# All contraction tiles and the memory's values by Strassen's method in an fp32 decoder layer, its weight sums by DMA, and another order of its first loads

## The chip, the cores and the metric

The kernel runs on one core of one Trainium2 chip. The metric is the device time of one execution in microseconds (us): 1042.24 us, the median of three runs of the kernel before, which lay between 1041.75 and 1042.37. The engines that compute are TensorE (PE, with its weight load PEld), VectorE (DVE), ScalarE (ACT) and GpSimd (POOL); SyncE (SP) issues most transfers. Each engine runs its own queue of instructions in order, and semaphores tie the queues together.

## The reference

One decoder layer of 512 tokens of width 1024, all in float32: a half-step SwiGLU block (inner width 2816), a mixer, cross-attention into 256 memory tokens, and a second SwiGLU block, each followed by a residual and a layer norm.

```python
def _swiglu(h, w_in, w_out):
    gate, up = jnp.split(h @ w_in, 2, axis=-1)
    return (jax.nn.silu(gate) * up) @ w_out

def _memory_attention(h, mem, wq, wk, wv, wo):
    q = (h @ wq).reshape(b_, s_, XA_HEADS, XA_HEAD_DIM)
    k = (mem @ wk).reshape(b_, m_, XA_HEADS, XA_HEAD_DIM)
    v = (mem @ wv).reshape(b_, m_, XA_HEADS, XA_HEAD_DIM)
    s = jnp.einsum('bshd,bmhd->bhsm', q, k).astype(jnp.float32) * (XA_HEAD_DIM ** -0.5)
    p = jax.nn.softmax(s, axis=-1).astype(v.dtype)
    return jnp.einsum('bhsm,bmhd->bshd', p, v).reshape(b_, s_, D_MODEL) @ wo

# the layer
h = _layernorm(ALPHA * h + 0.5 * _swiglu(h, w_ffn1_in[l], w_ffn1_out[l]), ln1_g[l], ln1_b[l])
h = _layernorm(ALPHA * h + _parallel_mixer(...), ln2_g[l], ln2_b[l])
h = _layernorm(ALPHA * h + _memory_attention(h, mem, xa_wq[l], xa_wk[l], xa_wv[l], xa_wo[l]), ln3_g[l], ln3_b[l])
h = _layernorm(ALPHA * h + 0.5 * _swiglu(h, w_ffn2_in[l], w_ffn2_out[l]), ln4_g[l], ln4_b[l])
```

## The kernel before

**Three matmuls for one.** A float32 operand is split into a high part, rounded to the matmul's fast format, and the remainder as a low part. A product is then high times high, high times low, low times high: three matmuls that add up in one bank of the accumulator memory. Every weight block (128 rows of 1024 floats, 512 KB) is fetched by `wblock` (L76): SP issues the load into a tile `raw_...`, ACT casts it to `whi_...` (L67), DVE subtracts to get `wlo_...` (L68). There are seven buffers for the raw tiles, and seven for the high and low ones together. Activations are split in the same way.

**The stages, in the order of the program.** The first loads (L107 to L118) bring the eight pieces `x[k]` of the transposed input and the eight pieces `first[k]` of the first weights; all other work on PE waits for them. The FFN's first GEMM (`ffn`) makes gate and up by Strassen's method over the input's width, in matmuls of 256 columns. Its second GEMM (`strassen_gemm`, L317) has 22 contraction tiles of 128, held in six tiles `f1g0` to `f1g5` (`f2g...` in the second FFN). Twenty of them go through Strassen's method: five blocks for each half of the contraction (`KB1`, `KB2`), seven products of 5 blocks and 12 matmuls of 512 columns each, which accumulate in the banks u, v and w. The last two tiles are added by plain matmuls (`rest`, on the split tile `gs` and two weight blocks `ws`; 48 matmuls), and a bank x takes some of these. Seven products need sums of quarters on both sides: the left ones are made by DVE (`combine`, `left`), the right ones (t1, t2, t3, t4, sums of weight blocks) by transfers.

**The right sums** (class `Sums`, L268). POOL issues a transfer that copies a weight block to a scratch in DRAM, and a second one that adds another block to it on the way. A tiny POOL instruction (`seen`) that reads an instruction's result holds such a transfer back until that point of the program. For the first FFN all 20 copies and 20 adds are issued during its first GEMM (`step`); for the second one they are spread behind the 50 weight blocks of the mixer and the attention (`spread`, called through `behind`). They end there ahead of the last stage of the attention. In the output GEMM SP loads the sums like any weight block (`raw_f1t`, `raw_f2t`), without transfers of POOL beside it.

**The memory's values.** After the mixer and its layer norm come the keys of the memory (`pk`, `KM`) and then the values V = mem times wv (L899 to L914): two halves of 512 columns, four weight blocks each, 12 matmuls of 512 columns per block, 96 in all, into banks `vm`; ACT and DVE split each bank into `VM`. The split memory `mT` is there already. The query GEMM (weights `wxq`) follows.

**What sets the order.** The code is written once, and a scheduler at build time lays out each engine's queue. PE's queue is in order, so that an instruction that waits holds everything behind it. The same is true of DVE's, where splits, sums and residual adds share one queue, and of POOL's, where the power for a layer norm (`rstd`, L177) stands among the transfers.

Of the kernel before, what the change touches and what calls it, by code (L numbers as in the profile page):

```python
# [34 lines left out]
def layer_kernel(ctx: ExitStack, tc: tile.TileContext, a, out):  # L35
# [35 lines left out]

    last, behind = [None], []

    def wblock(src, name, stay=False):
        raw = raw4([P, 1024], f"raw_{name}")
        last[0] = nc.sync.dma_start(raw, src).ins  # L76
        if stay:
            both = b8([P, 2, 1024], F32R, f"ws_{name}")
            hi, lo = both[:, 0, :], both[:, 1, :]
        else:  # L80
            hi, lo = q4([P, 1024], f"whi_{name}"), q4([P, 1024], f"wlo_{name}")
        split(raw, hi, lo)
        for f in behind:
            f(hi)
        return hi, lo
# [22 lines left out]
    for k in range(KT):  # L108
        x = xf[k // 4][:, k % 4, :]
        nc.sync.dma_start(x, a["xT"][k])  # L110
        raw = raw4([P, 512], f"rawx{k}")
        (nc.scalar if k == 0 else nc.sync).dma_start(raw, a["first"][k])
# [152 lines left out]
    KB1, KB2 = [0, 1, 4, 5, 8], [2, 3, 6, 7, 9]  # L265
    NB = len(KB1)

    class Sums:  # L268


        def __init__(self, wsrc, name):
            self.w, self.name, self.T = wsrc, name, {}
            self.copies = [(p, b) for b in range(NB) for p in ("t1", "t3", "t2", "t4")]
            self.adds = list(self.copies)

        def copy(self, behind, of=("t1", "t3", "t2", "t4"), engine=None):

            todo = [c for c in self.copies if c[0] in of]
            if todo:
                p, b = todo[0]  # L280
                self.copies.remove(todo[0])
                T = self.T[p, b] = scr.tile([P, 1024], F32, name=f"{self.name}{p}{b}")
                with tc.issue_after(behind):
                    (engine or nc.sync).dma_start(T, self.w[p in ("t3", "t2"), (KB2 if p in ("t2", "t4") else KB1)[b]])

        def add(self, behind):

            if self.adds and self.adds[0] in self.T:
                p, b = self.adds.pop(0)
                x = {"t1": lambda: self.w[1, KB1[b]], "t3": lambda: self.w[1, KB2[b]],  # L290
# [4 lines left out]
        def spread(self, hi, over, count=[0]):  # L295

            total = 8 * NB
            n0, n1 = (total * (count[0] + i) // over for i in range(2))
            count[0] += 1
            for n in range(n0, min(n1, total)):  # L300
                seen = st.tile([P, 1], F32, tag="seen", name="seen")
                ins = nc.gpsimd.tensor_tensor(out=seen, in0=hi[:, 0:1].bitcast(F32), in1=mhalf[:, 0:1], op=ALU.mult).ins
                if self.copies and (n % 2 == 0 or n < 4):
                    self.copy(ins, engine=nc.gpsimd)
                else:
                    self.add(ins)

        def step(self, q, n):
# [3 lines left out]
            for _ in range(3 if n in (2, 4) else 2):  # L312
                self.add(ins)
            for _ in range(3 if n < 4 else 2):
                self.copy(ins, engine=nc.gpsimd)

    def strassen_gemm(wsrc, gt, S_, alpha, g, b, eps, name, final, pre):  # L317
        tiles = None
        stats = [st.tile([P, 2, 6], F32, tag=f"stats{t}", name=f"stats{t}", bufs=1) for t in range(NT)]
        lo, hi = slice(0, 256), slice(256, 512)  # L320
        quarter_ = {n: [gt[i][:, :, sl], gt[i + 2][:, :, sl], gt[4][:, i:i + 2, sl]]
                    for n, i, sl in (("a11", 0, lo), ("a12", 1, lo), ("a21", 0, hi), ("a22", 1, hi))}
        for n, i, sl in (("a12", 2, lo), ("a22", 2, hi)):
            quarter_[n][2] = gt[4][:, i:i + 2, sl]

        def left(p):

            T = []
            for i, x in enumerate(quarter_[p]):
                n = x.shape[1]  # L330
                t = (b8([P, 4, 2, 256], F32R, f"{name}{p}{i}") if n == 4
                     else wp.tile([P, 2, 2, 256], F32R, tag="raw", name=f"{name}{p}{i}", bufs=7))
# [4 lines left out]
        def combine(o, x, y, op):  # L337
            for i in range(3):
                nc.vector.tensor_tensor(out=quarter_[o][i], in0=quarter_[x][i], in1=quarter_[y][i], op=op)

        def right(p, stay=0):

            direct = {"b11": (0, KB1), "b21": (0, KB2), "b22": (1, KB2)}
            for i in range(NB):
                src = wsrc[direct[p][0], direct[p][1][i]] if p in direct else S_.T[p, i]
                yield wblock(src, f"{name}{p}{i}", i < stay)

        def block(t, i, w, T, ps, opens, ends):

            tsl = slice(t * P, (t + 1) * P)  # L350
            for j in range(2):
                k = 2 * i + j
                csl = slice(j * 512, (j + 1) * 512)
                ah, al = T[k][0][:, tsl], T[k][1][:, tsl]
                for n, (x, y) in enumerate(((ah, w[0]), (ah, w[1]), (al, w[0]))):
                    nc.tensor.matmul(ps, x, y[:, csl], start=opens and k == 0 and n == 0,  # L356
                                     stop=ends and j == 1 and n == 2, skip_group_check=True)

        def product(T, p, ps, opens):
            for i, w in enumerate(right(p)):  # L360
                for t in range(2):
                    block(t, i, w, T, ps[t], opens, False)
# [9 lines left out]
        assert not S_.copies and not S_.adds  # L372
        u, v, w = ([mm_ps(f"{name}{n}{t}") for t in range(2)] for n in "uvw")
        L = left("a11")
        s1 = b8([P, 2, 4, 256], F32, f"{name}s1")
        s1_ = sm.tile([P, 2, 256], F32, tag="s1", name=f"{name}s1_", bufs=2)
        quarter_["s1"] = [s1[:, 0], s1[:, 1], s1_]
# [15 lines left out]
        product(L, "b21", w, True)  # L393
        combine("a12", "a12", "a11", ALU.add)
        L = left("a12")

        T = b8([P, 2, 2, S], F32R, f"{name}gs")
        split(gt[5][:, :2, :], T[:, :, 0, :], T[:, :, 1, :])
        gs = [[(T[:, k, 0, sl], T[:, k, 1, sl]) for k in range(2)] for sl in (lo, hi)]
        product(L, "b22", v, False)  # L400
        ws = [wblock(wsrc[hf, 2 * NB], f"{name}{hf}_{2 * NB}", stay=True) for hf in range(2)]
# [9 lines left out]
        def rest(t, hf, ps, opens, scale):  # L411

# [653 lines left out]
```

## Time and profile before

| | value |
|---|---|
| median of three runs | 1042.24 us |
| the profiled execution | 1043.13 us, of which its span 1041.4 us |
| granted clock of TensorE, mean | 0.997 |
| ACT busy, of the span | 504.3 us (48%) |
| POOL busy, of the span | 95.0 us (9%) |
| bytes read and written in DRAM | 168.34 MB and 44.04 MB |
| POOL's transfers for the right sums | 30 from the second FFN's and 30 from the first FFN's weights, and 20 more between scratches |

The span is the profiled part of the execution, from its first instruction to its last; the 1.7 us around it are counted in the time, and taken as the same for both kernels. "L356" is line 356 of the kernel. In rows of a timeline the first number is the start, the second the time from the first start to the last end of the run of instructions in the row; in square brackets stands the time that the engine sat idle before, and what released it. A matmul's own duration in a row includes its drain; what one costs in a stream is the distance between two starts.

### The profile page before, as it was taken

The page shows a single profiled execution, that of the slowest core. Times are in us where ns is not written, and L with a number is a line of the kernel's source. Part 1 is how long each engine was busy: PE and PEld are TensorE (multiplying, and loading weights), DVE is VectorE, ACT ScalarE, POOL GpSimd, SP SyncE. Part 2 cuts the span into 40 slices and gives each one's busy share as a digit, 9 for nine tenths or more (in the row PEclk, how much of TensorE's full clock was granted, in tenths as well). Part 3 has the DMA queues.
Part 4 walks back from the last instruction along what each step waited for, and adds up shares of the span by engine and source line. Part 5 has one row for each costly group of instructions (what it writes and reads, how often), then busy time and mean ns, then how long its engine had stood idle before and what let it go on. Part 6 is the DMA issues. An engine that isn't in the chain of part 4 may idle for free. (4 is left out here: it accounts for less than half of the span.)

```text
span 1041.4 us, 17704 instructions
## 1 busy us (share of the span) xinstructions
PE 1025.7 (98%) x6910; PEld 929.4 (89%) x6910; DVE 825.4 (79%) x1334; ACT 504.3 (48%) x857; POOL 95.0 (9%) x167
## 2 busy tenths in 40 slices
PE   9999999999999999999999999999999999999996
PEld 7999999998887888879888988889999999988884
DVE  6999888789898545786786356589988888889795
ACT  5656555566554331334324345226555555566530
POOL 0112211200000111102303110010000000000000
PEclk9999999999999999999999999999999999999998
DMA  9377786585665446553929871403233332436751
GB/s 364 143 236 230 222 254 212 148 247 158 216 192 182 142 155 169 148 168 82 292 72 314 273 162 41 141 22 107 97 101 122 103 101 65 139 102 202 235 189 41
DMA packets 43300, 171.59 MB, mean 165 GB/s; under 512 B 6096, under 2 KB 7376, under 8 KB 40016
## 3 DMA queue, kind: packets, MB, share of 16 engines
q1 hardware_dynamic: 38592, 128.25, 36.9%
q0 software_dynamic: 4480, 41.95, 15.9%
q8 instruction: 54, 0.88, 0.3%
q10 hardware_dynamic: 144, 0.26, 0.1%
q14 instruction: 30, 0.25, 0.1%
HBM read 168.34 MB, written 44.04 MB: 204 GB/s over the span
## 5 line engine op out<-in xcount | busy, mean ns | idle before, releaser
L177 POOL TENSOR_TENSOR rstd<-ve,mhalf 128x1 f32<-128x1 f32 x16 | 14.8, 922 | 536.1 <-DVE ve L175 536.1
L538 PE MATMUL f1u<-xt,qf1s 128*128 128x256 f32 x480 | 60.7, 283 | 0.0
L538 PE MATMUL f2u<-xt,qf2s 128*128 128x256 f32 x480 | 60.7, 283 | 0.0
L538 PEld LDWEIGHTS f1u<-xt,qf1s 128*128 128x128 f32 x480 | 59.0, 192 | 0.0
L538 PEld LDWEIGHTS f2u<-xt,qf2s 128*128 128x128 f32 x480 | 59.0, 192 | 0.0
L68 DVE TENSOR_TENSOR wlo_wv<-raw_wv,whi_wv 128x1024 fp32r<-128x1024 f32 x12 | 14.7, 1224 | 23.8 <-PE pq L57 8.5
L538 PE MATMUL f1u<-xT,qf1a 128*128 128x256 f32 x240 | 32.1, 283 | 0.0
L538 PE MATMUL f2w<-xoT,qf2a 128*128 128x256 f32 x240 | 32.1, 283 | 0.0
L538 PE MATMUL f2u<-xoT,qf2a 128*128 128x256 f32 x240 | 32.1, 283 | 0.0
L538 PE MATMUL f1w<-xT,qf1a 128*128 128x256 f32 x240 | 32.1, 283 | 0.0
L538 PE MATMUL f1v<-xt,qf1s 128*128 128x256 f32 x240 | 30.7, 283 | 0.0
L538 PE MATMUL f1u<-xt,qf1a 128*128 128x256 f32 x240 | 30.6, 283 | 0.0
L538 PE MATMUL f1v<-xT,qf1s 128*128 128x256 f32 x240 | 30.4, 283 | 0.0
L538 PE MATMUL f2v<-xt,qf2s 128*128 128x256 f32 x240 | 30.4, 283 | 0.0
L538 PE MATMUL f2v<-xoT,qf2s 128*128 128x256 f32 x240 | 30.4, 283 | 0.0
L538 PE MATMUL f2u<-xt,qf2a 128*128 128x256 f32 x240 | 30.4, 283 | 0.0
L538 PEld LDWEIGHTS f1w<-xT,qf1a 128*128 128x128 f32 x240 | 30.3, 192 | 0.1
L538 PEld LDWEIGHTS f1u<-xT,qf1a 128*128 128x128 f32 x240 | 30.2, 192 | 0.0
L538 PEld LDWEIGHTS f2w<-xoT,qf2a 128*128 128x128 f32 x240 | 30.2, 192 | 0.0
L538 PEld LDWEIGHTS f2u<-xoT,qf2a 128*128 128x128 f32 x240 | 30.2, 192 | 0.0
L538 PEld LDWEIGHTS f1v<-xt,qf1s 128*128 128x128 f32 x240 | 29.6, 192 | 0.1
L538 PEld LDWEIGHTS f1u<-xt,qf1a 128*128 128x128 f32 x240 | 29.6, 192 | 0.0
(458 smaller groups left out, 3220.3 us busy)
## 6 DMA issues: line engine op xcount, KB each, us to landing
f1t<-in_w1out POOLq DMA_DIRECT2D x30, 512.0 KB, 8.2
f2t<-in_w2out POOLq DMA_DIRECT2D x30, 512.0 KB, 6.6
raw_f1t<-f1t SPq DMA_DIRECT2D x20, 512.0 KB, 4.1
raw_f2t<-f2t SPq DMA_DIRECT2D x20, 512.0 KB, 3.9
raw_f2g<-in_w2in SPq DMA_DIRECT2D x17, 512.0 KB, 3.7
raw_f2u<-in_w2in SPq DMA_DIRECT2D x17, 512.0 KB, 3.7
raw_f1u<-in_w1in SPq DMA_DIRECT2D x15, 512.0 KB, 7.2
raw_f1b<-in_w1out SPq DMA_DIRECT2D x15, 512.0 KB, 4.8
```

What stands on the lines that cost most here:

```text
L68: nc.vector.tensor_tensor(out=lo, in0=src, in1=hi.bitcast(F32), op=ALU.subtract)
L177: nc.gpsimd.tensor_tensor(out=rstd, in0=ve, in1=mhalf[:, 0:1], op=ALU.pow)
L538: nc.tensor.matmul(o, q[:, w, wsl], x[k][r], start=opens and k == 0 and n == 0, stop=ends and k == 3 and n == 2, skip_group_check=True)
```

## The change

1. **First loads.** SP issues `first[k]` ahead of `x[k]`; before it was `x[k]` first, and `first[0]` was issued from ACT's queue. In DVE's queue the low part of `first[0]` now stands ahead of the cast of `x[0]`, and PE's four products of the high parts stand at the front.
2. **The FFN's output GEMM.** All 22 tiles go through Strassen's method. There is a sixth block for each half of the contraction that has one tile: the two halves of weight block 10. `rest`, `gs`, `ws` and bank x are gone. A product is 66 matmuls, a GEMM 462 (before 468).
3. **Right sums.** Each sum has six blocks, the last one half as large. t1, t2 and t3 are made during the FFN's first GEMM as before, 2 adds and 2 copies a step; the six copies and six adds of t4 now stand inside the output GEMM, one behind every second weight block (`one_behind`, `pace`). In the mixer and the attention the sums for V come first (8 copies, 8 adds), then those of the second FFN as far as the stages reach, behind four of five weight blocks and behind none in the stage of V; what is left by then is issued in the second FFN. POOL issues 116 of them in place of 80.
4. **The memory's values.** V goes through Strassen's method: tokens, contraction and columns are halved, seven products of 2 weight blocks and 6 matmuls a block, 84 in place of 96. The 8 weight blocks become 14, eight of which are sums read back from the scratch. The memory is loaded a second time in float32 (`memf`, 1 MB), DVE makes four sums on it and ACT and DVE four splits of those, and the results pass through the copies c11, c12 and c22.

```diff
-        nc.sync.dma_start(x, a["xT"][k])
         raw = raw4([P, 512], f"rawx{k}")
-        (nc.scalar if k == 0 else nc.sync).dma_start(raw, a["first"][k])
+        nc.sync.dma_start(raw, a["first"][k])
+        nc.sync.dma_start(x, a["xT"][k])
...
-    KB1, KB2 = [0, 1, 4, 5, 8], [2, 3, 6, 7, 9]
+    FFN_BLOCKS = [0, 1, 4, 5, 8, (10, 0)], [2, 3, 6, 7, 9, (10, 1)]
...
+        def actions(self):
+            c, a, seq = len(self.copies), len(self.adds), []
+            while a:
+                if c and a - c < 4:
+                    seq.append(self.copy)
+                    c -= 1
+                else:
+                    seq.append(self.add)
+                    a -= 1
+            return seq
...
+    todo_behind, pace = [], [0, 1, 2]
+    def one_behind(hi):
+        pace[0] += 1
+        if todo_behind and pace[0] * pace[1] % pace[2] < pace[1]:
+            seen = st.tile([P, 1], F32, tag="seen", name="seen")
+            todo_behind.pop(0)(nc.gpsimd.tensor_tensor(out=seen, in0=hi[:, 0:1].bitcast(F32), in1=mhalf[:, 0:1],
+                                                       op=ALU.mult).ins)
...
-        assert not S_.copies and not S_.adds
+        todo_behind.extend(S_.actions())
+        pace[:] = 0, 1, 2
...
-        ws = [wblock(wsrc[hf, 2 * NB], f"{name}{hf}_{2 * NB}", stay=True) for hf in range(2)]
-        def rest(t, hf, ps, opens, scale):
-            block(t % 2, 0, ws[hf], gs[t // 2], ps, opens, True)
-            add(t, hf, ps, scale)
         for t in range(2):
-            rest(t, 0, w[t], False, False)
-            rest(t, 1, v[t], False, False)
+            for hf, ps in enumerate((w[t], v[t])):
+                add(t, hf, ps, False)
+                stats_of(t, hf)
...
         for t in range(2):
             add(2 + t, 1, u[t], False, ALU.subtract)
-            rest(2 + t, 1, mm_ps(f"{name}x{t}"), True, False)
+            stats_of(2 + t, 1)
         for t in range(2):
             for i, x in enumerate(T4):
-                block(t, i, x, L, u[t], False, False)
-            rest(2 + t, 0, u[t], False, True)
+                block(t, i, x, L, u[t], False, i == nb - 1)
+            add(2 + t, 0, u[t], True)
+            stats_of(2 + t, 0)
...
-    behind.append(lambda hi: sums2.spread(hi, 50))
+    sums_v = Sums(a["wv"], "vm", [0, 1], [2, 3])
+    todo_behind += sums_v.actions() + sums2.actions()
+    pace[:] = 0, 4, 5
...
+    mem_sum("s1", "a21", "a22", ALU.subtract)
+    mem_sum("a21", "a11", "a21", ALU.subtract)
+    mem_sum("a11", "s1", "a11", ALU.subtract)
+    mem_sum("a12", "a12", "a11", ALU.add)
+    vu, vv, vw = (mm_ps(f"vm{n}") for n in "uvw")
+    mem_product(vu, mem_left("a11", (0, 0)), "b11", True, False)
+    c11 = part_of_v("c11", vu)
+    mem_product(vv, mem_left("s1"), "t1", True, False)
+    c22 = part_of_v("c22", vv)
+    mem_product(vu, mem_left("a11"), "t2", False, False)
+    c12 = part_of_v("c12", vu)
+    mem_product(vw, mem_left("a12", (1, 0)), "b21", True, True)
+    nc.vector.tensor_tensor(out=c11, in0=c11, in1=vw, op=ALU.add)
+    values_done(0, 0, c11)
+    mem_product(vv, mem_left("a12"), "b22", False, True)
+    nc.vector.tensor_tensor(out=c12, in0=vv, in1=c12, op=ALU.subtract)
+    values_done(0, 1, c12)
+    mem_product(vu, mem_left("a21"), "t3", False, False)
+    nc.vector.tensor_tensor(out=c22, in0=c22, in1=vu, op=ALU.subtract)
+    values_done(1, 1, c22)
+    mem_product(vu, mem_left("a22", (1, 1)), "t4", False, True)
+    values_done(1, 0, vu)
+    pace[:] = 0, 4, 5
```

Three places in the queues. A row is the line, the operation, what it writes and reads, and the shape; the number behind a name's underscore only counts the program's tiles.

**DVE at the start of the first FFN's output GEMM, before.** `f1a110` and `f1a111` are the low parts of the first product's left operand (of `f1g0` and `f1g2`), `wlo_f1b112` is the low part of its third weight block, and `f1g5` is the last tile of the inner activations.

```order
L525 TENSOR_TENSOR f1g5_275<-f1sg_2616,f1u_2621 128x256
L68 TENSOR_TENSOR wlo_f1b112_2992<-raw_f1b112_2989,whi_f1b112_2991 128x1024
L525 TENSOR_TENSOR f1g5_275<-f1sg_2687,f1u_2692 128x256
L68 TENSOR_TENSOR f1a110_2942<-f1g0_270,f1a110_2942 128x4x256
L68 TENSOR_TENSOR f1a111_2945<-f1g2_272,f1a111_2945 128x4x256
```

The same place after the change; `f1a113` is the left operand of the new half block.

```order
L534 TENSOR_TENSOR f1g5_275<-f1sg_2606,f1u_2611 128x256
L68 TENSOR_TENSOR f1a110_2936<-f1g0_270,f1a110_2936 128x4x256
L534 TENSOR_TENSOR f1g5_275<-f1sg_2677,f1u_2682 128x256
L68 TENSOR_TENSOR f1a111_2939<-f1g2_272,f1a111_2939 128x4x256
L68 TENSOR_TENSOR f1a113_2945<-f1g5_275,f1a113_2945 128x256
L68 TENSOR_TENSOR wlo_f1b112_2994<-raw_f1b112_2991,whi_f1b112_2993 128x1024
```

The first left operand now stands ahead of the third weight block's low part, which was in front of it.

**DVE in the stage of V, before.** `wlo_wv10` is the low part of the first weight block of the second column half, `vm00` a bank of the first.

```order
L68 TENSOR_TENSOR wlo_wv03_5994<-raw_wv03_5991,whi_wv03_5993 128x1024
L68 TENSOR_TENSOR wlo_wv10_6018<-raw_wv10_6015,whi_wv10_6017 128x1024
L68 TENSOR_TENSOR wlo_wv11_6040<-raw_wv11_6037,whi_wv11_6039 128x1024
L68 TENSOR_TENSOR VM0_5923<-vm00_5925,VM0_5923 128x512
L68 TENSOR_TENSOR wlo_wv12_6061<-raw_wv12_6058,whi_wv12_6060 128x1024
L68 TENSOR_TENSOR VM1_5924<-vm01_5926,VM1_5924 128x512
```

After the change, the front of the stage: the last key `KM1` (from the last product ahead of V), the last of the four sums on `memf`, the splits of s1 and a11, and then the first weight blocks of the sums t1 and t2 (`wvt10` to `wvt20`).

```order
L68 TENSOR_TENSOR KM1_5119<-pk_5975,KM1_5119 128x256
L942 TENSOR_TENSOR memf_6004<-memf_6004 128x4x128
L68 TENSOR_TENSOR vls1_6040<-vs1_6006,vls1_6040 128x4x128
L68 TENSOR_TENSOR vla11_6069<-memf_6004,vla11_6069 128x4x128
L68 TENSOR_TENSOR wlo_wvt10_6046<-raw_wvt10_6043,whi_wvt10_6045 128x1024
L68 TENSOR_TENSOR wlo_wvt11_6058<-raw_wvt11_6055,whi_wvt11_6057 128x1024
L68 TENSOR_TENSOR wlo_wvt20_6075<-raw_wvt20_6072,whi_wvt20_6074 128x1024
```

And its end, with the last weight blocks (t3 and t4) and the results; `c22` reads the bank u (`vmu`) into which the last product, t4, adds next.

```order
L966 TENSOR_TENSOR c11_6038<-c11_6038,vmw_6013 128x512
L68 TENSOR_TENSOR wlo_wvb221_6143<-raw_wvb221_6140,whi_wvb221_6142 128x1024
L68 TENSOR_TENSOR wlo_wvt30_6161<-raw_wvt30_6158,whi_wvt30_6160 128x1024
L68 TENSOR_TENSOR VM0_6002<-c11_6038,VM0_6002 128x512
L969 TENSOR_TENSOR c12_6096<-vmv_6012,c12_6096 128x512
L68 TENSOR_TENSOR wlo_wvt31_6173<-raw_wvt31_6170,whi_wvt31_6172 128x1024
L68 TENSOR_TENSOR wlo_wvt40_6188<-raw_wvt40_6185,whi_wvt40_6187 128x1024
L68 TENSOR_TENSOR VM0_6002<-c12_6096,VM0_6002 128x512
L972 TENSOR_TENSOR c22_6067<-c22_6067,vmu_6011 128x512
L68 TENSOR_TENSOR wlo_wvt41_6200<-raw_wvt41_6197,whi_wvt41_6199 128x1024
```

Between the last key and `c22` stand 11 splits of a weight block and, with `c22`, 10 operations on 512 columns; where these rows lie, the weight blocks were before split with a result between them now and then.

**POOL ahead of the attention's layer norm, before.** A `seen` reads the high part of a weight block, and the transfer behind it is held to that; the layer norm's first `rstd` is the last row.

```order
L302 TENSOR_TENSOR seen_6771<-whi_xo0_0_6767,mhalf_264 128x1
L293 DMA f2t24_6120<-f2t14_6023 64x2048
L302 TENSOR_TENSOR seen_6808<-whi_xo0_1_6804,mhalf_264 128x1
L293 DMA f2t44_6242<-f2t24_6120 64x2048
L177 TENSOR_TENSOR rstd_6971<-ve_6969,mhalf_264 128x1
```

The same place after the change; `whi_f2g0` and `whi_f2u0` are the first weight blocks of the second FFN, whose loads SP issues there.

```order
L322 TENSOR_TENSOR seen_7028<-ws_xo1_1_7025,mhalf_264 128x1
L281 DMA f2t23_7030<-in_w2out 16x8192
L322 TENSOR_TENSOR seen_7037<-ws_xo1_2_7034,mhalf_264 128x1
L290 DMA f2t22_6609<-f2t12_6226 64x2048
L322 TENSOR_TENSOR seen_7056<-whi_f2g0_7052,mhalf_264 128x1
L281 DMA f2t14_7058<-in_w2out 16x8192
L322 TENSOR_TENSOR seen_7066<-whi_f2u0_7062,mhalf_264 128x1
L290 DMA f2t13_6880<-in_w2out 64x2048
L174 TENSOR_TENSOR rstd_7100<-ve_7098,mhalf_264 128x1
```

The transfers behind the first and second weight block of the output projection are gone from there, and others now stand behind its last blocks and behind the second FFN's first two.

180 lines of the change are left out of this document (96 added, 84 removed).

## The prediction

> **What bounds the kernel now.** I read the page's busy times first, then the chain that ended last, then windows of the stages that the change touches, and last the timelines at the places where PE stops.
>
> ```profile
> PE 1025.7 (98%) x6910; PEld 929.4 (89%) x6910; DVE 825.4 (79%) x1334; ACT 504.3 (48%) x857; POOL 95.0 (9%) x167
> PE 10%; DVE 0%; DVEq 0%; issue 0%
> PE f2u L356 5%; PE f2v L356 3%; PE f2w L356 2%; PE f2x L356 0%; DVE h L183 0%; DVE h L180 0%; DVE stats L415 0%; DVE h L367 0%; DVEq L1062 0%; DVE mv L173 0%; DVE ve L175 0%
> ```
>
> PE is busy in 98% of the span, and the part of the chain that the page follows runs through PE's matmuls of the last output GEMM. So a matmul that goes is time won, as long as what feeds PE keeps up. The price of a matmul comes from the old stage of V, where PE never stopped:
>
> ```profile
> L909 PE MATMUL vm<-whi_wv,mT x32: 389/389/396, 557.5 to 578.6; 128*128 128x512 f32 x32
> L911 PE MATMUL vm<-whi_wv,mT x32: 389/389/389, 558.0 to 579.1; 128*128 128x512 f32 x32
> 557.00:580.00 23.00, 23.00 (x108) 19.24 (x107) 12.58 (x13) 10.88 (x14) 5.89 (x13) 1.00 1.04 348
> ```
>
> The first and the last of its 96 matmuls start 21.6 us apart, so one costs 21.6 / 95 = **0.227 us**. The window's columns are PE, PE's loads, DVE, ACT, POOL, the granted clock, the DMA share and GB/s: DVE works 12.6 of 23 us, while the DMA engines are full.
>
> **The FFN's output GEMMs: matmuls, and the stall at the start.** 468 matmuls become 462, in two FFNs: 12 x 0.227 = **-2.72 us** if nothing takes PE's place.
>
> ```profile
> 230.63 0.40 PE L356 MATMUL f1u<-wlo_f1b,f1a 128*128 128x512 f32 x1
> 231.77 0.73 PE L356 MATMUL f1u<-whi_f1b,f1a 128*128 128x512 f32 x2 [0.74 <-DVE f1a L68]
> 924.39 0.40 PE L356 MATMUL f2u<-wlo_f2b,f2a 128*128 128x512 f32 x1
> 925.53 0.73 PE L356 MATMUL f2u<-whi_f2b,f2a 128*128 128x512 f32 x2 [0.75 <-DVE f2a L68]
> 229.03 1.22 DVE L68 TENSOR_TENSOR wlo_f1b<-raw_f1b,whi_f1b 128x1024 fp32r<-128x1024 f32 x1
> 230.16 0.41 DVE L525 TENSOR_TENSOR f1g<-f1sg,f1u 128x256 f32<-128x256 f32 x1
> 230.49 2.36 DVE L68 TENSOR_TENSOR f1a<-f1g,f1a 128x1024 fp32r<-128x1024 f32 x2
> ```
>
> At the start of each GEMM PE steps from 230.63 to 231.77 and from 924.39 to 925.53: 1.14 in place of 0.227, a loss of 0.91. It waits for the low part of the first left operand, and DVE had the third weight block's low part in front of that (229.03 to 230.16 by the starts, 1.13). The change puts the weight block behind. That is more than the loss, so both stalls go: **-1.83 us** (at worst 0, if DVE reaches this place later by as much). Late next is the second left operand, which follows by two operations and is needed four matmuls on at the earliest.
>
> DVE's own load in this stage grows. Prices by the distance of starts: 1.13 for 1024 columns, 0.33 for 256 (230.16 to 230.49), 0.61 for 512 (567.88 to 568.49, below). Added per FFN: 1.5 blocks' splits (1.7), seven pieces of left operands (2.3), four pieces of sums (1.3); gone: `gs` (1.1) and two residual adds (1.2): +3.0.
>
> ```profile
> 231.50:323.00 91.50, 91.23 (x406) 75.61 (x407) 83.30 (x92) 49.95 (x53) 1.99 (x2) 1.00 0.61 194
> 924.40:1014.70 90.30, 89.55 (x395) 73.85 (x394) 82.54 (x89) 48.89 (x51) 1.85 (x2) 1.00 0.62 198
> 1011.97 2.72 PE f2x L356 x12
> ```
>
> DVE goes from 82.5 of 90.3 us to some 85.5 of 89.4: 96%. It still fits, with the buffers of three and a half blocks between it and PE, but not everywhere. The weakest place is in front of the t4 product. Before, PE had the 12 matmuls into bank x there (2.72 us in the chain) while DVE emptied bank u; now t4 goes into u at once. The add of 512 columns (0.69) has only the last three matmuls of the other bank (0.68) beside it, and what remains is the matmul's drain (0.39 - 0.23 = 0.16) and what DVE is behind by. I take 0.25 per FFN, **+0.5 us** (0 to 2: at the upper end the whole add and a share of the last splits stand open).
>
> **The memory's values.** Ideally 84 x 0.227 = 19.1 in place of 21.8. But DVE has the longer list.
>
> ```profile
> 567.88 0.69 DVE L68 TENSOR_TENSOR VM<-vm,VM 128x512 fp32r<-128x512 f32 x1 [0.57 <-ACT VM L67]
> 568.49 1.22 DVE L68 TENSOR_TENSOR wlo_wv<-raw_wv,whi_wv 128x1024 fp32r<-128x1024 f32 x1
> 545.00:557.00 12.00, 12.00 (x102) 11.93 (x101) 10.80 (x19) 6.58 (x12) 5.73 (x8) 1.00 0.80 253
> 557.71 0.37 ACT L67 CAST KM<-pk 128x256 fp32r<-128x256 f32 x1 [1.56 <-PE pk L58]
> ```
>
> Let the first matmul of V start at T. DVE is at work 10.8 of the 12 us ahead of it, so the new sums on `memf` can't be finished early. The last key's cast on ACT ends about T + 0.6 (557.71 + 0.37 against 557.5). From there DVE's queue holds the key (0.33), ten operations of 512 columns (6.1) and 11 splits (11 x 1.13 = 12.4) up to and with `c22`: T + 19.4. The low part of `wvt10` is the fifth operation; it is done at T + 0.6 + 0.33 + 3 x 0.61 + 1.22 = T + 4.0, while PE has used its first 12 matmuls and one more at T + 2.95: a stall of 1.05. `c11`, `c12` and `c22` each wait for a product that PE ends later by this, so I put it on DVE's list: `c22` at T + 20.5. Only then can t4's 12 matmuls enter bank u: 20.5 + 2.72 + drain of about 0.2 = T + 23.4, against 21.8: **+1.6 us**, though 12 matmuls are gone. If DVE's waits are hidden, it is T + 22.3, +0.5; if PE waits for nothing at all, -2.7, which DVE's list excludes. The other way, loads that come late decide:
>
> ```profile
> raw_wxq<-in_wq SPq DMA_DIRECT2D x8, 512.0 KB, 13.0
> raw_wv<-in_wv SPq DMA_DIRECT2D x6, 512.0 KB, 5.6
> 530.00:545.00 15.00, 15.00 (x86) 12.54 (x85) 13.21 (x28) 4.11 (x10) 1.54 (x2) 1.00 0.04 11
> q1 hardware_dynamic: 38592, 128.25, 36.9%
> q0 software_dynamic: 4480, 41.95, 15.9%
> ```
>
> SP's queue moved 128.25 MB in 36.9% of 1041.4 us on all 16 DMA engines: 1.57 us for a block of 512 KB. Old V fetched 8 blocks while POOL's sums filled the engines, and `raw_wv` landed 5.6 us after its issue. Now no sum is issued here, but 14 blocks take 22.0 us of all engines: nearly the whole stage. The 1 MB of `memf` and the first blocks can come ahead of it, where the share was 0.04 in 530 to 545. I take no loss, and one late block, 4 us (the 5.6 less what a buffer ahead covers), as the upper end.
>
> **The attention's layer norm (LN3).** Two sums of POOL now lie beside the loads of the second FFN's first blocks.
>
> ```profile
> 677.82 0.69 DVE L517 TENSOR_TENSOR f2s<-raw_f2u 128x512 f32<-128x512 f32 x1 [3.19 <-DMA raw_f2u<-in_w2in]
> 678.43 0.68 DVE L243 SCALAR_TENSOR_TENSOR h<-h,xops 128x512 f32<-128x512 f32 x1
> 682.88 0.63 PE L195 MATMUL trh<-ident,h 128*128 128x128 f32 x4 [0.69 <-DVE h L183]
> raw_f2u<-in_w2in SPq DMA_DIRECT2D x5, 512.0 KB, 4.5
> ```
>
> DVE waits 3.19 us for `raw_f2u`, the residual add `h` stands behind it in the queue, and PE waits 0.69 for the norm of that `h`; whatever delays it further adds to this wait one for one. POOL's 80 transfers took 15.9% of 1041.4 = 166 us, 2.07 each. One such beside the load moves the chain DVE, `h`, `trh` by 0 to 2.1; two by 4.1 at most. I take half of one, **+1.0 us**, because the landing of 4.5 us holds queueing that may absorb some. In the Trainium skill, "DMA: Bandwidth & Descriptors", section "Queues, rings and completion order", each DMA engine takes turns between the queues that have work, a packet at a time. By that rule a load meets one sum packet for each of its own: the load's 1.57 us would double, this term would be +1.6, and the sum 0.6 above mine. The landings of 13.0 us beside sums and 4.5 us without agree with sharing, though more of SP's loads were queued in the first.
>
> **The first loads.**
>
> ```profile
> 4.91 0.43 DVE L67 CAST xT<-xf 128x512 fp32r<-128x512 f32 x1 [3.90 <-DMA xf<-in_xT]
> 5.11 0.62 ACT L67 CAST qx<-rawx 128x512 fp32r<-128x512 f32 x1 [2.44 <-DMA rawx<-in_first]
> 5.98 0.68 DVE L68 TENSOR_TENSOR qx<-rawx,qx 128x512 fp32r<-128x512 f32 x1
> 6.72 0.50 PE L58 MATMUL first<-xT,qx 128*128 128x512 f32 x1
> ```
>
> Before, PE's stream is closed from its third matmul on, at 6.72, as if it had started without gaps at 6.72 - 2 x 0.23 = 6.27. Now `first[0]` lands first, near 4.9; ACT casts it to 5.5, DVE's low part takes to about 6.15, and only then comes the cast of `x[0]` (0.43): start at 6.6, with four high products to cover the rest. **+0.35 us** (-0.4, if the first transfer lands earlier now that none is issued beside it, to +0.9).
>
> Transfers in the first FFN's first GEMM become fewer by those of t4; nothing waited there, so nothing is won.
>
> **Sum:** -2.72 - 1.83 + 0.5 + 1.6 + 1.0 + 0.35 = -1.1. From the profiled execution's 1043.13 (span 1041.4, 1.7 around it, taken as unchanged) that gives 1042.0. That execution lies 0.89 above the median of 1042.24, so the forecast for a median is **1041.1 us**. About 0.2% (2.1 us) is what a measurement of this kernel can tell from no change, so this is "the same".
>
> **Rivals.**
> *Cheaper V and hidden tails.* PE is fed as the buffers allow: V costs +0.5, LN3 and the t4 start nothing: -2.72 - 1.83 + 0.5 + 0.35 = -3.7, 1038.5. For it speaks that DVE and ACT are free for 10 of 23 us in the old V; against it, the order of DVE's list.
> *The output GEMM falls behind: slower.* Its 12 sums now share the DMA engines with 42 loads. In a product of 15 us SP fetches 5.5 blocks' worth and POOL makes 1.7 transfers: 5.5 x 1.57 + 1.7 x 2.07 = 12.2 us of all engines, 81%, where the window shows 0.61. PE has about five raw blocks ahead (the left operands hold the others of the seven buffers), 5 x 2.72 us less some 2.2 for the block's split: **11.4 us of landing time is the point from which it decides**. `raw_wxq` took 13.0 beside sums, but at a share of 1.04; that speaks against it. With DVE at 96% nothing is caught up: 1.7 us for each of two blocks, about 3.5 per FFN: 1041.1 + 7 = 1048.
> *The change does little of what it says*, because DVE at 96% in the output GEMMs hands PE each block just in time and the time of the 12 matmuls goes into waits: the sum without its first term, 1041.1 + 2.7 = 1043.8. It ends within the measurement.
>
> **How the numbers follow.** Forecast 0.45 (1041.1), cheaper 0.25 (1038.5), little gained 0.11 (1043.8), slower 0.19 (1048). Faster by over 0.2% means under 1040.2: nearly all of the cheaper case and the lower end of the forecast, 0.23 + 0.08 = 0.31. Slower means over 1044.3: nearly all of the slower case, and a late load in V, 0.18 + 0.03 = 0.21. The rest is 0.48. The range goes from the cheaper case, half a microsecond lower for the bound of the first loads (1038.0), to the forecast with the late load of V or with one FFN falling behind (1041.1 + 4, rounded up: 1045.2). The forecast's own range is 1039.7 to 1042.9.
>
> **What would show it.** Right: no step over 0.4 us at the start of the two output GEMMs, matmuls of 512 columns fewer by 24; in V two stalls of about 1 us, by `wlo_wvt10` and by `c22`, and DVE nearly closed between them; one longer wait for `raw_f2u` ahead of `trh`. Wrong: loads in the output GEMMs that land after 10 us or more with PE waiting for `whi_f1b` or `whi_f2t` (the slower case); V with 20 us or less (the cheaper one); stalls spread over the output GEMMs that end at DVE (the one with little gained).

## The result, and the profile after

| | before | after |
|---|---|---|
| median of five runs | 1042.32 us | 1048.65 us (1045.56 to 1049.13) |
| ratio | 1 | 1.0055 (95% interval 1.0043 to 1.0066) |
| the profiled execution, its span | 1043.13, 1041.4 us | 1045.56, 1043.8 us |

The changed kernel is slower by 6.3 us, outside the range of the prediction. Its profiled execution is the shortest of the five; the others took 1048.2 to 1049.1. What the trace of 1045.56 shows is told first, and the 3 us to the others with the first experiment.

The page of the changed kernel, with each engine's busy time, and its line on POOL's transfer queue (packets, MB, share of 16 DMA engines):

```profile
PE 1023.6 (98%) x6886; PEld 924.7 (89%) x6886; DVE 842.4 (81%) x1377; ACT 517.9 (50%) x892; POOL 156.8 (15%) x232
q0 software_dynamic: 6784, 54.53, 21.2%
```

PE's busy time fell by 2.1 us and its matmuls from 6910 to 6886, the 24 that the prediction named, while the time rose: something else came. To find it, the span is cut at the first matmul of each stage. The table has, in us, the kernel before, two traces of the changed one (the second is from e1), and some of the experiments that follow: e3 and e4 are built on the kernel before, e5 to e9 on the changed one.

| stage | before | e3 | e4 | after, 1st | after, 2nd | e5 | e6 | e7 | e9 |
|---|---|---|---|---|---|---|---|---|---|
| until the first matmul on loaded data | 5.78 | 4.97 | 5.24 | 5.25 | 5.24 | 5.31 | 5.25 | 5.30 | 5.29 |
| first products | 22.43 | 22.44 | 22.41 | 22.64 | 22.77 | 21.86 | 22.26 | 22.20 | 22.63 |
| FFN 1, first GEMM | 201.72 | 201.89 | 201.72 | 201.85 | 201.87 | 201.88 | 201.84 | 201.84 | 201.84 |
| FFN 1, output GEMM | 111.43 | 110.63 | 110.71 | **107.82** | **108.50** | 108.38 | 108.59 | 108.16 | 108.38 |
| mixer and keys | 216.15 | 216.16 | 216.16 | 216.80 | 216.75 | 216.76 | 216.78 | 216.74 | 216.77 |
| V, queries, attention | 90.47 | 90.47 | 90.51 | **92.56** | **92.66** | 92.73 | 92.61 | 90.46 | 89.43 |
| output projection, norm (LN3) | 49.75 | 49.78 | 49.84 | **51.89** | **54.45** | 49.61 | 49.65 | 49.58 | 49.59 |
| FFN 2, first GEMM | 225.95 | 225.95 | 225.95 | 225.96 | 225.95 | 226.38 | 225.95 | 225.96 | 226.42 |
| FFN 2, output GEMM | 106.93 | 106.93 | 106.93 | **105.65** | **105.40** | 105.39 | 105.61 | 105.65 | 105.65 |
| from the last matmul's start to the end | 10.73 | 8.13 | 13.66 | **13.36** | **13.35** | 13.35 | 8.04 | 7.95 | 8.04 |
| span | 1041.36 | 1037.36 | 1043.13 | 1043.79 | 1046.94 | 1041.65 | 1036.58 | 1033.83 | 1034.06 |

In the second trace the output GEMMs are shorter by 2.93 and 1.53 us, and the mixer's stage is longer by 0.60; some 0.4 of that are four small matmuls (`trh`) of a late norm, which now stand behind the mixer's first matmul. V lost 2.2, the norm behind the attention 2.1 and 4.7, and the end of the program 2.6.

e3 and e4 show how far one trace of the kernel before can be trusted, since they leave its code as it is up to the second FFN. They agree with it to 0.2 us in each stage up to there but two. They start earlier, and their first output GEMM takes 110.63 and 110.71 us in place of 111.43. The same place in the timelines of the kernel before and of e4:

```profile
324.36 0.63 PE L195 MATMUL trh<-ident,h 128*128 128x128 f32 x4 [0.91 <-issue]
323.08 0.63 PE L195 MATMUL trh<-ident,h 128*128 128x128 f32 x4 [0.20 <-issue]
```

The wait of 0.91 us in the middle of the GEMM is 0.20 in e4, and 0.14 in e3. So 0.7 to 0.8 of the 2.93 us, and PE's earlier start, differ between executions of the same code and can't be put down to the change. Against e3 and e4 the output GEMMs with the mixer won 3.1 us in the second trace.

**The output GEMMs.** A timeline of PE of the changed kernel, at the places of the two stalls of 0.91 us:

```profile
229.97 0.40 PE L367 MATMUL f1u<-wlo_f1b,f1a 128*128 128x512 f32 x1
230.21 0.90 PE L367 MATMUL f1u<-whi_f1b,f1a 128*128 128x512 f32 x3
925.01 0.40 PE L367 MATMUL f2u<-wlo_f2b,f2a 128*128 128x512 f32 x1
925.25 0.89 PE L367 MATMUL f2u<-whi_f2b,f2a 128*128 128x512 f32 x3
```

No step between matmuls is over 0.25 us here; both stalls are gone. In front of t4 PE lost 0.35 us in the second FFN (0.19 of idle time and the drain of the matmul ahead). Loads that come late were a rival; the changed kernel's transfers, in the windows of the two GEMMs (number, size, median time to landing), say no:

```profile
raw_f1b<-in_w1out SPq DMA_DIRECT2D x10, 512.0 KB, 7.2
raw_f2b<-in_w2out SPq DMA_DIRECT2D x10, 512.0 KB, 7.5
```

They land later than before (4.5 in the first GEMM). The slowest took 10.3 us, which is under the 11.4 from which PE would have waited by the prediction's estimate, and no wait of PE in the two GEMMs ends at a load.

**V.** Timelines of PE and DVE of the changed kernel; V's first matmul starts at 554.36:

```profile
557.11 1.22 DVE L68 TENSOR_TENSOR wlo_wvt<-raw_wvt,whi_wvt 128x1024 fp32r<-128x1024 f32 x1
558.38 0.50 PE L938 MATMUL vmv<-wlo_wvt,vls 128*128 128x512 f32 x1 [0.89 <-DVE wlo_wvt L68]
572.99 0.50 PE L938 MATMUL vmu<-wlo_wvt,vla 128*128 128x512 f32 x1 [0.68 <-DVE wlo_wvt L68]
574.58 0.68 DVE L972 TENSOR_TENSOR c<-c,vmu 128x512 f32<-128x512 f32 x1
575.41 0.47 PE L938 MATMUL vmu<-whi_wvt,mT 128*128 128x512 f32 x1 [1.00 <-ACT whi_wxq L67]
```

There are three large waits. Two stand where the prediction put them: at the first block of t1 (558.38, 4.0 us into the stage), whose low part DVE ended at 558.33 after work without a gap from 554.96 on, and at t4, which has to wait until `c22` has read bank u. The third, at t3's second block, was not forecast. The row of the wait at t4 names an ACT instruction, which came at about the same time; `c22` ends at 574.58 + 0.68 = 575.26, 0.15 ahead of the matmul. Between the first and the last of these waits DVE stands still for 1.1 us in all. The stage took 23.9 us against 21.8.

**The norm behind the attention (LN3).** Timelines of the changed kernel, POOL's, SP's, DVE's and PE's row:

```profile
672.24 0.79 POOL L290 DMA_DIRECT2D f2t<-in_w2out  x1
672.27 0.33 SPq L502 DMA_DIRECT2D raw_f2u<-in_w2in  x1
678.92 0.69 DVE L526 TENSOR_TENSOR f2s<-raw_f2u 128x512 f32<-128x512 f32 x1 [5.35 <-DMA raw_f2u<-in_w2in]
683.98 0.63 PE L192 MATMUL trh<-ident,h 128*128 128x128 f32 x4 [2.85 <-DVE h L180]
```

POOL issues a sum 0.03 us ahead of SP's load of `raw_f2u`; its other sums of this stage had landed by 668.4. The load takes 6.6 us (4.5 before), DVE waits 5.35 in place of 3.19, and PE 2.85 in place of 0.69: 2.2 us more, one for one.

**The end.** The last rows of the changed kernel's timeline, and two windows behind them (PE, PE's loads, DVE, ACT, POOL, granted clock, DMA share, GB/s):

```profile
1033.95 1.41 DVE L180 SCALAR_TENSOR_TENSOR h<-h,rstd,B 128x512 f32<-128x512 f32 x2
1034.72 0.99 SPq L419 DMA_DIRECT2D out<-h  x2
1035.00:1041.00 6.00, 0.00 (x0) 0.00 (x0) 0.36 (x1) 0.00 (x0) 0.00 (x0) 0.50 0.23 87
1041.00:1043.00 2.00, 0.00 (x0) 0.00 (x0) 0.00 (x0) 0.00 (x0) 0.00 (x0) 0.50 0.00 0
```

The two last stores are issued from 1034.7 on and have landed by 1037.4, and nothing works any more, but the span goes on to 1043.8. In the trace's records of the queues themselves, which these views leave out, POOL stands in an instruction DRAIN; the end of the program puts one into each engine's queue. Its record starts at 1032.75, with POOL's last work (the norm's `rstd`, up to 1033.78), and takes 10.25 us; all other engines wait for it. In the kernel before the same DRAIN starts at 1033.01 and takes 7.56. SP is done at 1037.7, and at 1037.9 in the kernel before. So the span's end was set by POOL already before the change, and the change made it 2.7 us longer.

### The profile page after: what moved, and what is told of

Same layout as the page of the kernel before. It is cut to its first block, busy times and chain, and to the rows that moved or that the text cites. A ratio compares the mean times of both kernels' runs of the same rounds, so it can differ in the third digit from the quotient of the medians.

```text
span 1043.8 us, 17894 instructions
## 1 busy us (share of the span) xinstructions
PE 1023.6 (98%) x6886; PEld 924.7 (89%) x6886; DVE 842.4 (81%) x1377; ACT 517.9 (50%) x892; POOL 156.8 (15%) x232
## 3 DMA queue, kind: packets, MB, share of 16 engines
q0 software_dynamic: 6784, 54.53, 21.2%
## 5 line engine op out<-in xcount | busy, mean ns | idle before, releaser
L307 POOL TENSOR_TENSOR seen<-qf1a,mhalf 128x1 f32<-128x1 f32 x10 | 5.6, 555 | 180.2 <-ACT qf1a L67 137.0
L307 POOL TENSOR_TENSOR seen<-qf2a,mhalf 128x1 f32<-128x1 f32 x10 | 5.3, 537 | 180.2 <-ACT qf2a L67 180.2
```

The costliest lines, as they stand in the source:

```text
L307: ins = nc.gpsimd.tensor_tensor(out=seen, in0=q[:, 0, 0:1].bitcast(F32), in1=mhalf[:, 0:1], op=ALU.mult).ins
```

## The experiments

**e1: the changed kernel again.**

> The changed kernel once more, for a second trace. Its profiled execution took 1045.56 us, four others 1048.2 to 1049.1, and those four show a lower mean clock (0.993 to 0.994 against 0.995). Theory D (the end): after SP's last wait POOL still works off a DRAIN, 10.25 us in the profiled execution against 7.56 in the kernel before, and in the longer executions this DRAIN is longer by about 3 us: TensorE then sits idle at a low clock for longer, which is the lower mean. Then a trace of 1048 to 1049 has the same stages as the first one to 0.3 us each, and 13 us of DRAIN. Rival C (clock): the pause ahead of the attention's layer norm, 3.2 us in the first trace, is longer there and the clock falls behind it; the stage of the output projection grows by about 3 us. Rival L (loads): an output GEMM of an FFN grows by about 3 us.

1048.71 us (1048.31 to 1050.47), ratio 1.0069 (1.0056 to 1.0081). The trace is of a typical execution, and of the three explanations rival C is right: the DRAIN is 10.25 us as in the first trace, the output GEMMs are alike to 0.7 us, and the output projection's stage has grown from 51.9 to 54.5. The timeline of this kernel at that place, and windows behind it:

```profile
673.14 0.33 SPq L502 DMA_DIRECT2D raw_f2u<-in_w2in  x1
680.83 0.69 DVE L526 TENSOR_TENSOR f2s<-raw_f2u 128x512 f32<-128x512 f32 x1 [6.39 <-DMA raw_f2u<-in_w2in]
685.89 0.65 PE L192 MATMUL trh<-ident,h 128*128 128x128 f32 x4 [3.90 <-DVE h L180]
688.48 0.63 PE L225 MATMUL xops<-whi_xo,oT 128*128 128x512 f32 x1
688.90 0.63 PE L223 MATMUL xops<-ws_xo,oT 128*128 128x512 f32 x1
686.00:688.00 2.00, 2.00 (x10) 1.83 (x10) 1.10 (x2) 0.67 (x2) 0.00 (x0) 0.59 0.00 0
688.00:690.00 2.00, 2.00 (x6) 1.53 (x5) 0.83 (x2) 0.99 (x2) 0.00 (x0) 0.56 0.00 0
690.00:692.00 2.00, 2.00 (x10) 1.65 (x9) 1.97 (x5) 0.59 (x1) 0.46 (x1) 1.00 0.00 0
```

The load took 7.7 us here, PE's pause was 3.90 in place of 2.85, and behind it the granted clock is 0.59 and 0.56 for 4 us: matmuls start 0.42 us apart (688.48, 688.90) in place of 0.227. The longer pause costs 1.05 us more than in the first trace; the rest of the stage's growth of 2.56, some 1.5, is put down to the slow clock. In the first trace the clock behind the pause of 2.85 us is 1.00. Why the load took 7.7 us here and 6.6 there, beside the same sum, stays open.

In the Trainium skill, "TensorE: Matmul & The Clock Gate", Part 1, TensorE's clock goes to one half after an idle window of about 3.4 us. The traces agree in part: 2.85 us of waiting kept the clock, 3.90 and (in e2) 4.33 lost it. But these rows of e2, the last two matmuls ahead of its pause and a window in it, show the clock falling sooner:

```profile
680.35 0.39 PE L227 MATMUL xops<-whi_xo,oT 128*128 128x512 f32 x1
680.57 0.39 PE L228 MATMUL xops<-wlo_xo,oT 128*128 128x512 f32 x1
682.00:684.00 2.00, 0.00 (x0) 0.00 (x0) 1.93 (x6) 0.00 (x0) 0.76 (x1) 0.78 0.00 0
```

A mean of 0.78 over 2 us is full speed up to about 683.1 and half behind it, 2.2 us after PE's last matmul ended (680.96). So the length of a wait alone does not say whether the clock falls, and where the limit lies isn't shown.

**e2, e3: the last norm off POOL.**

```diff
-        nc.gpsimd.tensor_tensor(out=rstd, in0=ve, in1=mhalf[:, 0:1], op=ALU.pow)
+        if final:
+            nc.scalar.activation(rstd, ve, AF.Sqrt)
+            nc.vector.reciprocal(rstd, rstd)
+        else:
+            nc.gpsimd.tensor_tensor(out=rstd, in0=ve, in1=mhalf[:, 0:1], op=ALU.pow)
```

On the changed kernel:

> The changed kernel with one edit: the power of the last FFN's layer norm is taken by ACT and DVE (square root, reciprocal) in place of POOL, so that POOL's last instruction is a transfer of the t4 sums, some 30 us before the end. Theory D: the DRAIN starts there and is over before SP's last wait; the end after PE's last matmul shrinks from 13.4 to about 8 us and the time to 1040 us (1045.56 - 5.3), in all executions alike, as the longer ones lose their longer DRAIN. If the DRAIN has nothing to do with the transfers, or starts only when all engines are done: 1045 to 1049 as before.

On the kernel before:

> The kernel before with the same edit alone. Theory D: its DRAIN of 7.56 us outlasts SP's last wait by 2.7 us, so 1042.3 becomes 1039.6. Without D: 1042.3, or some tenths off either way for the norm itself.

e3: 1039.73 us, ratio 0.9981 (0.9972 to 0.9990), where 1039.6 was expected. The DRAIN starts at 700.91, with POOL's last work (the `rstd` of LN3), takes 7.64 us and hides; the end shrinks from 10.73 to 8.13. e2: 1045.56 us (1.0033; 1.0020 to 1.0046), 3.2 us less than the changed kernel and not 8.7. The end did shrink as forecast, from 13.36 to 8.39, but the expectation that the 3 us of the longer executions lie in the DRAIN was wrong: they lie in the norm behind the attention, whose pause was 4.33 us here (stage 55.5).

**e4: transfers without bytes.**

```diff
+            seen = st.tile([P, 1], F32, tag="seen", name="seen")
+            ins = nc.gpsimd.tensor_tensor(out=seen, in0=quads[order[6], "a11"][:, 0, 0:1].bitcast(F32),
+                                          in1=mhalf[:, 0:1], op=ALU.mult).ins
+            for n in range(36):
+                T = scr.tile([1, 128], F32, name=f"tiny{n}")
+                with tc.issue_after(ins):
+                    nc.gpsimd.dma_start(T, a["x"][n:n + 1, :128])
```

> The kernel before with 36 further transfers of 512 bytes that POOL issues in the second FFN, where it has nothing else to do; they are read by nothing. They bring the number of POOL's transfers from 80 to 116 at almost no bytes. If the DRAIN goes by the number of transfers: 10.2 us in place of 7.56, time 1045. If it goes by bytes or by packets (2304 packets more made 2.7 us in the changed kernel, here it is at most some hundred): 7.6 to 8 us, time 1042.3 to 1042.7.

1045.34 us, ratio 1.0032 (1.0019 to 1.0044). The DRAIN takes 10.50 us. It goes by the number of transfers that POOL has issued in the program, and not by their bytes (41.97 MB in place of 41.95). Nor does it go by packets, though the 36 made 1152 of them and not some hundred, by the page's count of POOL's queue: with 5632 packets here the DRAIN is longer than with 6784 in the changed kernel. And it doesn't matter how long ago the transfers were: POOL had issued these by 788, over 240 us ahead of the DRAIN. POOL's DRAIN in all the traces:

| | POOL's transfers | DRAIN starts | takes |
|---|---|---|---|
| before | 80 | 1033.01 | 7.56 |
| after (both traces), e5 | 112 | 1032.75, 1035.91, 1030.62 | 10.25 |
| e4: before and 36 of 512 bytes | 116 | 1031.85 | 10.50 |
| e3: before, norm off POOL | 80 | 700.91 | 7.64 |
| e7, e10: norm off POOL | 96 | 956.90, 956.70 | 10.85, 10.52 |
| e2, e6, e8, e9: norm off POOL | 112 | 980.03, 974.57, 970.87, 972.37 | 12.38, 12.53, 13.03, 12.65 |

(10.25 - 7.56) / 32 and (10.50 - 7.56) / 36 give 0.084 and 0.082 us for each transfer. In the first four rows the record holds the 0.92 to 0.99 us of the `rstd` that POOL has still to do; what is left, 6.61, 9.23, 9.55 and 6.61 us, is 0.082 to 0.083 us for each of the 80, 112, 116 and 80 transfers, with no fixed part. Where the DRAIN starts in the middle of an output GEMM (the last two rows) it takes some 2 us longer, but is hidden there. POOL's last transfers are still under way then (in e6 the last lands at 982.47), as they are not in the other rows; whether that is the reason isn't shown. (The trace has 112 transfers of POOL after the change, where the text ahead of the prediction has 116.)

**e5: no sums around LN3.** One line, ahead of the attention's output projection:

```diff
+    pace[:] = 0, 0, 5
     ys, wx = [], []
```

> The changed kernel with one line more: no right sums are issued from the attention's output projection to the end of its layer norm; those left are issued in the second FFN's first GEMM. Theory S (a sum beside a load): one sum, issued just ahead of the load of raw_f2u, makes that load land some 2 us later, PE's pause ahead of trh grows from 1.1 to 3.2 us and more, and where it is over some 3.3 to 3.9 us the granted clock falls to about half for 4 us behind it. Without the sum the load lands in 4.5 us again, the pause is 1.1, the clock stays, the stage from the output projection to the second FFN takes 49.8 us again (51.9 to 55.5 with the sums) and the time is 1048.7 - 4.7 = 1044.0. If the raw_f2u load is late for another reason (the order of SP's queue, DVE): the stage keeps 52 to 55 us and the time 1046 to 1049.

1043.67 us, ratio 1.0014 (1.0005 to 1.0022). The timeline of this kernel at the same place:

```profile
672.25 0.33 SPq L502 DMA_DIRECT2D raw_f2u<-in_w2in  x1
676.64 0.69 DVE L526 TENSOR_TENSOR f2s<-raw_f2u 128x512 f32<-128x512 f32 x1 [3.09 <-DMA raw_f2u<-in_w2in]
681.69 0.63 PE L192 MATMUL trh<-ident,h 128*128 128x128 f32 x4 [0.59 <-DVE h L180]
```

The load lands after 4.4 us, PE waits 0.59, and the stage is 49.6 us as before the change. SP's load is issued at the same time as in the first trace (672.25 and 672.27), so the sums were the cause, and not its place in SP's queue. e5 takes five of them out of this stage; only the last was under way beside this load.

**e6, e7: both together, and plain V.**

> The edit of e5 together with the last layer norm off POOL. If both causes stand side by side: 1044.0 less the 5 us by which POOL's DRAIN outlasts SP's last wait: 1039.0, below the kernel before and at or a little below the kernel before with its norm off POOL (1039.7). What then remains of the change is -2.5 and -1.5 in the output GEMMs, -0.3 in the first loads, +2.2 in the stage of V. If one hides the other: 1041 to 1044.

> e6 with the memory's values as in the kernel before (plain, 96 matmuls, no sums for them; POOL issues 96 transfers). If the stage of V costs the 2.2 us that its window shows: 1039.0 - 2.2 = 1036.8, stage of V 21.8 us. If the sums for V also held up something else, it is less than 1036.5.

In e7 the code of V is the old one:

```diff
-    mem_product(vu, mem_left("a11", (0, 0)), "b11", True, False)
...
+    for hf in range(2):
+        ps = [mm_ps(f"vm{hf}{t}") for t in range(2)]
+        for blk in range(4):
+            hi, lo = wblock(a["wv"][hf, blk], f"wv{hf}{blk}")
...
-    todo_behind += sums_v.actions() + sums2.actions()
+    todo_behind += sums2.actions()
```

e6: 1038.38 us, ratio 0.9965 (0.9953 to 0.9978). Neither cause hides the other: on top of e5's edit the norm off POOL takes another 5.3 us off, as much as the end shrinks by in the traces (13.35 to 8.04). e7: 1035.70 us, ratio 0.9940 (0.9927 to 0.9952); its stage of V is 21.79 us, and the 2.2 us come back (2.7 by the medians). Without the sums for V, POOL issues 96 transfers.

**e8, e9, e10: V by Strassen's method with time for DVE.** The queries of the first two heads stand between V's products:

```diff
     c22 = part_of_v("c22", vv)
+    xq(0)
...
     values_done(0, 1, c12)
+    xq(1)
...
-    xq(0)
-    xq(1)
     scores(0)
```

> e6 with Strassen's method for V kept, but the first four query products of PE put between V's products (after t1 and after b22), so that DVE has time for its list. If V's loss is DVE's list (PE waited 3.8 us in that stage): the waits go, the stage of V and the queries together take 12 matmuls less than before (41.5 us from V's first matmul to the first score in place of 44.2 before and 46.4 after), and the time is 1039.0 - 3.8 = 1035.2 or up to 1 us more. If V's loads are the limit instead, PE waits for raw_wv in other places and the time stays at 1038 to 1039.

> e8 with one difference: behind the weight blocks of the queries that stand between V's products right sums are issued again, so that three sums fewer are left to the second FFN. In e8 the second output GEMM took 1.7 us more than in e6 and e7, with pauses of PE ahead of t3's and t4's blocks. If the late sums cause that, the GEMM takes 105.6 us again and the time is 1035.0. If it is chance or the new order itself: 1036 to 1037, and V by Strassen's method brings nothing over plain V (1035.7).

> The kernel of e7 once more, on the same chip as e9, for the comparison of V by Strassen's method with plain V: 1035.7 as before. e9 under it by over 1 us: the method is worth it where DVE has time. Within 1 us: it is not, in this kernel.

e8: 1036.60 us (0.9942; 0.9929 to 0.9956). e9: 1035.88 (0.9941; 0.9926 to 0.9955), with `pace[:] = 0, 4, 5` ahead of each of the two calls and 0 again behind it; a second difference from e8 is `pace[:] = 0, 1, 1` behind V, a sum behind every weight block in place of four of five. e10, the kernel of e7 measured beside e9: 1036.35 (0.9945; 0.9932 to 0.9958). e8 lies 0.4 us above its expected range, e9 0.9 above what was expected. In the stage of e8 two waits of PE over 0.2 us are left, in place of three:

```profile
557.48 0.50 PE L942 MATMUL vmv<-wlo_wvt,vls 128*128 128x512 f32 x1 [0.28 <-DVE wlo_wvt L68]
559.54 0.39 PE L56 MATMUL pxq<-moT,whi_wxq 128*128 128x256 f32 x1 [0.37 <-ACT whi_wxq L67]
```

So DVE's list was the limit of V. But from V's first matmul to the output projection it is 89.43 us in e9 against 90.46 with plain V: 1.0 us of the 2.7 that 12 matmuls are worth. The same two pauses in e9 (0.28 and 0.40 of idle time, and 0.16 of drain ahead of each) cost 1.0 us of the rest; where the last 0.7 went stays open. By the medians, V by Strassen's method can't be told from plain V. In e8 the second output GEMM took 107.3 us, in e9 105.65; but plain V, too, had 106.6 in e10 and 105.65 in e7 with the same code, so e9 does not settle whether the late sums did it.

e7 (with e10), e8 and e9 are the fastest of these kernels, 0.6% under the kernel before, and can't be told from each other. 0.2% of that comes from the norm off POOL alone (e3).

## Why the prediction was wrong

Two steps failed: the size of the LN3 term, and the end of the program, which the sum took as fixed. The forecast was 1041.1 us, a typical execution took 1048.7, which is 7.6 more. By the stages of the second trace 3.7 of that lie in the LN3 term, 2.6 at the end, 0.6 in V, and -0.2 in the rest. The other 0.9 is what the profiled execution of the kernel before took over its median; the forecast took it off, and no stage of the change can be charged with it.

- **The matmuls and the stall of the output GEMMs: right in mechanism, nearly in size.** Forecast -2.72 - 1.83 + 0.5 = -4.05. Measured with the mixer's stage: -3.9 against the first trace of the kernel before, in which the wait for `trh` at 324 helps by chance, and -3.1 against e3 and e4. The 24 matmuls and both stalls went. Of the 0.9 us that are missing, 0.6 stand in the mixer's stage; for the rest the cause stays open.
- **V: right in its mechanism and nearly in its size.** Forecast +1.6, with waits at `wlo_wvt10` and in front of t4, DVE nearly closed between them; measured +2.1 and +2.2, with one wait more. e8 shows DVE's list as the cause.
- **LN3: the mechanism was right, the size was not.** This is the largest part of the miss. The step "I take half of one, +1.0 us", with bounds from 0 to 2.1 for one sum, measured +2.1 where the clock stayed and +4.7 in a typical execution. Two things were missed. The load was late by 2.1 to 3.6 us, more than the 2.07 of a sum by itself. And PE's pause was added to an existing one without asking how long it would be in all: 3.9 us, long enough for the clock to fall. The rule on turns between queues that the prediction cites from the Trainium skill gave +1.6 for this term, nearer than my choice, and still too little.
- **The end: a term that the sum did not have.** "From the profiled execution's 1043.13 (span 1041.4, 1.7 around it, taken as unchanged)" took all that lies behind the last matmul as fixed as well. The sum had no term for what 32 more transfers cost POOL itself: +2.6 us of DRAIN. The chain of waits on the page ends at the last store and doesn't show it; the span of the kernel before, which went on for some 4 us behind the store's landing, did.
- **The first loads: no effect shown.** +0.35 forecast. The first FFN's Strassen products start at 27.9 and 28.0 us against 28.20 before, but at 27.4 and 27.6 in e3 and e4, whose first loads are those of the kernel before. `first[0]` landed early enough for ACT's cast to start at 3.43, not at 4.9 as the working had it.
- **The rival that named 1048** came close to the measured time by luck. Its mechanism, an output GEMM that falls behind because of late loads, did not occur: the medians were 7.2 and 7.5 us to landing, the slowest load 10.3, under its 11.4, and both GEMMs got shorter.

With both errors out of the way (no sums around LN3, and the last norm off POOL on both sides), e6 against e3 is what the change is worth: 1038.38 against 1039.73, -1.35, where the sum without LN3 gives -2.1. The intervals of their ratios overlap (0.9953 to 0.9978, 0.9972 to 0.9990), so that this alone is not told from nothing. e7 against e3 is the same without V's new method: 1035.70 against 1039.73, -4.0 (-3.5 by the spans of the two traces), with intervals that are apart; that is close to the -4.05 forecast for the output GEMMs.

## What to carry to other kernels

A transfer that POOL issues has a price at the end of the program, 0.08 us each here, however small and however early: count them, or let POOL finish its last instruction early, so that its DRAIN lies beside other work (2.5 us of 1042.2 in the kernel before). When a wait gets longer, ask for its whole length: a pause of PE of 2.9 us cost itself, one of 3.9 some 1.5 us more. Take more than one trace of the kernel before: one wait of it that came and went was 0.7 us of what looked like the gain of a stage. A transfer in the background is cheap only where no load with a waiting engine is issued beside it.

## What the runs showed of the hardware that was not expected

Besides the DRAIN by number of transfers: POOL's smallest instruction can stand for 7 us. The changed kernel's timeline of POOL, two of DVE's rows beside it, and the window of the same time:

```profile
246.24 6.90 POOL L322 TENSOR_TENSOR seen<-whi_f1t,mhalf 128x1 f32<-128x1 f32 x1 [0.97 <-ACT whi_f1t L67]
248.13 1.22 DVE L68 TENSOR_TENSOR wlo_f1t<-raw_f1t,whi_f1t 128x1024 fp32r<-128x1024 f32 x1
249.60 1.22 DVE L347 TENSOR_TENSOR f1g<-f1s,f1g 128x1024 f32<-128x1024 f32 x1
246.00:253.00 7.00, 7.00 (x33) 5.79 (x32) 7.00 (x7) 2.78 (x4) 6.76 (x1) 1.00 0.81 294
```

The instruction reads and writes one number in each partition; of the 83 in this trace all but the two of 6.90 us take 0.2 to 2.7, most of them under 0.8. Here DVE was busy for all 7 us of the window, with splits and sums that read two tensors each, and the second FFN's output GEMM has the same again (6.90 at 941). In the two output GEMMs 20 of the 22 `seen` end 0.1 us behind the start of an instruction of DVE, and the other two when DVE falls idle: POOL seems to get its turn between two of DVE's instructions. Why it was passed over several times in a row here isn't shown. In the Trainium skill, "GPSIMD Engine Reference", section "Specifications", POOL shares its way to the on-chip memory with DVE and contends with DVE's instructions of two such inputs; the rows agree, but no run here took DVE's work away to show it. It holds back the t4 sums by that time, which nobody waited for.
